# Forward substitution with a block's 32 columns spread over four groups of partitions

## The chip, the cores and the metric

The kernel runs on one core of one Trainium2 chip. The metric is device time in microseconds of one execution of the whole program. Work is done by TensorE (PE), VectorE (DVE), ScalarE (ACT), GpSimd (POOL) and SyncE (SP, which here only issues transfers); each works through its own queue in order, and they wait for one another by semaphores.

## The reference

One layer on an input of 1024 rows and 2048 columns, all in float32. A normalised input goes through one projection, whose columns feed two groups of heads; their outputs are joined, projected again, added to the input and normalised. The part that the change touches is in the gated delta rule: for every head and every chunk of 64 positions a unit lower triangular system is solved.

```python
g = -exp(a_log) * softplus(a_raw + dt_bias); beta = sigmoid(b_raw)
kb, vb = k * beta, v * beta                      # chunks of 64 positions, 8 heads of 128
gc = cumsum(g); decay = exp(gc_i - gc_j) on and below the diagonal
L = strictly_lower((kb @ k.T) * decay)           # 64 x 64 for a head and chunk
rhs = concat([vb, kb * exp(gc)])
u, w = split(triangular_solve(L + I, rhs, lower, unit_diagonal))
attn = lower((q @ k.T) * decay)
# scan over chunks, state S of 128 x 128 for a head:
v_new = u - w @ S
o = (q * exp(gc)) @ S + attn @ v_new
S = S * exp(g_last) + (k * exp(g_last - gc)).T @ v_new
```

Its result is normalised per head and gated by silu of a projected `z`. The other group of heads mixes positions in chunks of 128 by a lower triangular matrix (`sp` below).

## The kernel before

The 1024 rows are worked in two halves (`hf`) of T = 512. TensorE is the engine that everything is arranged around: each projected tile of 128 columns is an accumulator `acc` of 128x512, built from four weight chunks. A chunk of weights is loaded by SP into `wr` (`w_chunk`, three buffers, asked for three chunks ahead), ScalarE casts it to a high half `wh` (line 136), VectorE subtracts to get the low half `wl` (line 137), and TensorE multiplies high by high, high by the input's low half, and low by high (lines 238, 239 and 241): 12 matmuls of 128x512 a chunk. A finished `acc` is evicted by VectorE (line 404) into `pc` (for q, k, v), `pcz` (for z) or `pczb`.

Everything else is written as generators ("tasks"). `tick()` runs every six matmuls; a task that yields n sleeps for n ticks. Within an engine the framework then orders the instructions by its own model of when they are ready; the queues that result are fixed in the program, and some are shown below in the section on the change.

The eight heads are four pairs in each half. For a pair, `task_pair` (lines 549 to 673) does the following. The 64x64 blocks L of its heads are in DRAM (`ld`). The two 32x32 diagonal blocks of each are inverted by forward substitution: 32 blocks on 32 partitions, L in `lu`, the growing inverse in `xu` that starts as the unit matrix (lines 557 to 559, on GpSimd). Step k takes a product into `tmp` (line 566) and subtracts it (line 568), for the 31-k rows below and the k+1 columns that are not zero; each step is followed by a yield of one tick. The inverse goes to DRAM (`xd`, line 572) and back as `tn` (line 574), in pieces of one row of a block, 128 bytes. Two waits stand around the steps: W_DMA1 = 6 ticks ahead of them and W_DMA2 = 18 behind.

The full inverse follows with small matmuls (`yp`, lines 584 and 593) and transposes of `tn` (line 578) into `tt`, then `up` and `wp` (lines 606, 611), and the scan over eight chunks for both heads (matmuls `p` and `ds` at lines 621 and 632; VectorE's `vz` and `state` at 624 and 633). For each head `at` (line 649) is added to `o` by VectorE (line 650), squares and a root follow, and `swap` carries the transposed result through DRAM by GpSimd's queue (`swapo`, lines 430 and 433); VectorE's line 672 gates it. The banks of `at`, `yp`, `up`, `wp` and of the other group's `sp` (line 744, evicted by VectorE's `s`, line 746) come from one set of two (`gen_bank`), so each waits for the eviction of the last but one.

Of the kernel before, what the change touches and what calls it, by code (L numbers as in the profile page):

```python
# [8 lines left out]
F32 = mybir.dt.float32  # L9
# [3 lines left out]
ALU = mybir.AluOpType  # L13
# [4 lines left out]
P = 128  # L18
# [5 lines left out]
NT = T // P  # L24
# [7 lines left out]
def kernel(ctx, tc, x_tok, x_t, w_in, w_v0, w_vb, w_out, conv_w, norm_w, a_log, dt_bias,  # L32
                       hn_w, sgu_w, sgu_b, wsp_t, b_sp, fn_w, out):
    nc = tc.nc
# [4 lines left out]
    big = pool("big", bufs=4)  # L39
    wk = pool("wk", bufs=2)  # L40
    sm = pool("sm", bufs=2)
    dr = pool("dr", bufs=2, space=DRAM)
# [8 lines left out]
    def bc(ap, shape):  # L51
        return ap.broadcast_to(shape)
# [21 lines left out]
    for c in range(2):  # L74
        r = slice(c * 64, (c + 1) * 64)
# [374 lines left out]
    W_RSTD = 1  # L450
    RS = 4
    W_FIRST = 6
    W_DMA1 = 6
    W_DMA2 = 18
    W_GATES = 12
    W_LN = 12
    W_EM = 5
# [33 lines left out]
    def task_q(hf, h, st, pr, acc):  # L491
# [32 lines left out]
        if hh == 1:  # L524
            spawn(task_pair(hf, h // 2, st, pr))
# [23 lines left out]
    def task_pair(hf, p, st, pr):  # L549
        gt, heads = st["gt"], pr["hd"]  # L550

        ld, xd = pr["ld"], pr["xd"]
        fs = big.tile([32, 2, 32, 32], F32, tag="b8", name=f"fs{hf}_{p}")
        lu, xu = fs[:, 0], fs[:, 1]
        ldv = ld.rearrange("h t (c s j) (z i) -> s z (h t c) j i", c=2, s=2, z=2)
        for s in range(2):
            nc.gpsimd.dma_start(lu[s * 16:(s + 1) * 16], ldv[s, s])
        nc.gpsimd.memset(xu, 0.0)
        nc.gpsimd.memset(xu.rearrange("u i j -> u (i j)")[:, ::33], 1.0)
        tmp = wk.tile([32, 256], F32, tag="fst", bufs=1, name=f"fst{hf}_{p}")  # L560
        yield W_DMA1

        for k in range(31):
            n, m = 31 - k, k + 1
            tv = tmp[:, 0:n * m].rearrange("u (i j) -> u i j", j=m)
            nc.vector.tensor_tensor(tv, bc(lu[:, k, k + 1:].unsqueeze(2), [32, n, m]),  # L566
                                    bc(xu[:, k:k + 1, 0:m], [32, n, m]), op=ALU.mult)
            nc.vector.tensor_tensor(xu[:, k + 1:, 0:m], xu[:, k + 1:, 0:m], tv, op=ALU.subtract)  # L568
            yield 1
        xdv = xd.rearrange("h t (c s j) i -> s (h t c) (j i)", c=2, s=2)  # L570
        for s in range(2):
            nc.sync.dma_start(xdv[s], xu[s * 16:(s + 1) * 16].rearrange("u i j -> u (i j)"))
        tn = wk.tile([P, 2 * NT, 32], F32, tag="tn", bufs=1, name=f"tn{hf}_{p}")
        nc.sync.dma_start(tn, xd.rearrange("h t p i -> p (h t) i"))
        yield W_DMA2

        for q in range(0, P, 32):
# [3 lines left out]
        for c in range(2):  # L581
            a, b = c * 64, c * 64 + 32
# [3 lines left out]
        for c in range(2):  # L586
            b = c * 64 + 32
            nc.scalar.activation(ys[b:b + 32], yp[b:b + 32], AF.Copy, scale=-1.0)
        yield 3
        for c in range(2):  # L590
            a, b = c * 64, c * 64 + 32
# [3 lines left out]
        for c in range(2):  # L595
            a, b = c * 64, c * 64 + 32
# [78 lines left out]
    def new_pair(hf, p):  # L675
        return dict(kq=big.tile([P, 2, 2, T], F32, tag="b8", name=f"kq{hf}_{p}"),
                    ld=dr.tile([2, NT, P, 64], F32, tag="ld", name=f"ld{hf}_{p}"),
                    xd=dr.tile([2, NT, P, 32], F32, tag="xd", name=f"xd{hf}_{p}"),
                    hd=[{}, {}])

    def group_a(hf, xs, st):
        pr = [None]

        def first_done(accs):
            if hf == 0:
                late_constants()
            st["gt"] = {}
            st["rb"] = x_rows(hf)
            spawn(task_gates(hf, accs[2:6], st, st["gt"]))
            pr[0] = new_pair(hf, 0)  # L690
            spawn(task_k(hf, 0, st, pr[0], accs[0]))
            spawn(task_q(hf, 0, st, pr[0], accs[1]))
        yield from first_tiles(hf, xs, st, first_done)
        for p in range(H // 2):
            def new(p=p):
                pr[0] = new_pair(hf, p)
            jobs = [(H, task_k, 0), (0, task_q, 0), (H, task_k, 1), (0, task_q, 1), (2 * H, task_v, 0), (2 * H, task_v, 1),
                    (3 * H, task_z, 0), (3 * H, task_z, 1)]
            for ct, task, i in jobs[2 if p == 0 else 0:]:
                def done(acc, ct=ct, task=task, h=2 * p + i, first=(i == 0 and ct == H)):  # L700
                    if first:
                        new()
                    spawn(task(hf, h, st, pr[0], acc))
                yield from project(hf, ct + 2 * p + i, xs, done)
# [375 lines left out]
```

## Time and profile before

| | us |
|---|---|
| median of three runs | 1774.84 (1774.63 to 1783.69) |
| the profiled execution | 1779.21 |
| its span | 1777.5 |
| TensorE busy | 1728.8 (97%) |
| VectorE busy | 1251.7 (70%) |
| ScalarE busy | 738.5 (42%) |
| GpSimd busy | 263.6 (15%) |

The granted clock of TensorE over the whole span is 0.992 of its full speed. A 128x512 matmul lasts 0.39 us by the record, but they overlap and start every 0.227 us, so that TensorE's pace is read from starts. "Idle" is time that an engine stood, with what released it.

### The profile page before, as it was taken

To read this page: it belongs to the slowest core of one execution; us is meant where nothing else is said; L and a number is where in the kernel's file an instruction comes from. 1 tells how busy PE (TensorE), PEld (TensorE's weight loads), DVE (VectorE), ACT (ScalarE), POOL (GpSimd) and SP (SyncE) were. 2 spreads that over 40 slices of the span, in tenths; PEclk is the share of its full clock that TensorE was granted. 3 is DMA by queue.
4 is the path that set the end of the run, shared out by engine and by line. 5 is a ranking of instruction groups with operands and counts; after the bars stand their busy time and mean duration, and the time that the engine had idled before them with its cause. 6 is when DMAs were issued, how large, how long until landed. Compare 5 with 4: busy or idle time off the path is not lost.

```text
span 1777.5 us, 27441 instructions
## 1 busy us (share of the span) xinstructions
PE 1728.8 (97%) x9334; PEld 1456.6 (82%) x9334; DVE 1251.7 (70%) x2945; ACT 738.5 (42%) x1678; POOL 263.6 (15%) x314
## 2 busy tenths in 40 slices
PE   9999999999999999998999999999989999999997
PEld 8778788888997788886878878889878888888885
DVE  7798797987747633757979789793863344767765
ACT  7543544445333222646344444532422234433454
POOL 4110131211201200203012112120020000200211
PEclk9999999999999999999999999999999999999998
DMA  7455445364458734426453645444884466766455
GB/s 239 128 134 145 108 124 144 91 169 133 132 172 260 258 108 126 130 69 153 126 134 92 164 106 149 134 116 117 248 277 133 118 188 199 223 191 193 144 190 190
DMA packets 190046, 277.99 MB, mean 156 GB/s; under 512 B 38064, under 2 KB 70864, under 8 KB 189648
## 3 DMA queue, kind: packets, MB, share of 16 engines
q1 hardware_dynamic: 185216, 263.60, 50.9%
q0 software_dynamic: 4544, 12.62, 3.0%
q8 instruction: 73, 1.20, 0.3%
q14 instruction: 69, 0.57, 0.1%
q10 hardware_dynamic: 144, 0.01, 0.0%
HBM read 220.54 MB, written 55.61 MB: 155 GB/s over the span
## 4 chain that ended last, share of the span: by engine, by line
PE 54%; DVE 9%; DMA 7%; ACT 2%; issue 2%; SPq 0%; POOL 0%; DVEq 0%; ACTq 0%; POOLq 0%
PE oa L1002 12%; PE acc L238 10%; PE acc L241 10%; PE acc L239 10%; PE vb L788 7%; DMA ws<-w_out 1%; DVE wl L137 1%; DVE cv L413 1%; DMA xres<-x_tok 1%; DMA wc_d<-ws 1%; DVE c L914 1%; PE p L621 1%; PE sp L744 1%; DMA wr<-w_in 1%; PE at L649 1%
## 5 line engine op out<-in xcount | busy, mean ns | idle before, releaser
L238 PE MATMUL acc<-xh,wh 128*128 128x512 f32 x1472 | 591.8, 402 | 1.0 <-ACT wh L136 1.0
L241 PE MATMUL acc<-xh,wl 128*128 128x512 f32 x1472 | 576.9, 392 | 7.5 <-DVE wl L137 7.5
L239 PE MATMUL acc<-xl,wh 128*128 128x512 f32 x1472 | 575.8, 391 | 0.0
L136 ACT CAST wh<-wr 128x512 fp32r<-128x512 f32 x368 | 225.7, 618 | 427.7 <-PE acc L239 270.6
L137 DVE TENSOR_TENSOR wl<-wr,wh 128x512 fp32r<-128x512 f32 x368 | 258.2, 704 | 154.2 <-ACT wh L136 151.2
L241 PEld LDWEIGHTS acc<-xh,wl 128*128 128x128 f32 x1472 | 277.1, 188 | 67.0 <-DVE wl L137 9.0
L238 PEld LDWEIGHTS acc<-xh,wh 128*128 128x128 f32 x1472 | 278.0, 189 | 57.7 <-issue 3.0
L239 PEld LDWEIGHTS acc<-xl,wh 128*128 128x128 f32 x1472 | 278.0, 189 | 51.5 <-issue 0.2
L1002 PE MATMUL oa<-who,a 128*128 128x512 f32 x864 | 267.9, 390 | 0.2 <-ACT who L136 0.2
L1002 PEld LDWEIGHTS oa<-who,a 128*128 128x128 f32 x864 | 162.6, 188 | 34.7 <-ACT who L136 0.6
L1002 PE MATMUL oa<-wlo,a 128*128 128x512 f32 x432 | 168.7, 390 | 0.6 <-DVE wlo L137 0.5
L137 DVE TENSOR_TENSOR wlo<-wro,who 128x512 fp32r<-128x512 f32 x108 | 79.4, 738 | 52.7 <-ACT who L136 52.2
L413 DVE SCALAR_TENSOR_TENSOR cv<-pc,cw,cv 128x511 f32<-128x511 f32 (+1 forms) x144 | 109.1, 758 | 9.6 <-ACT cv L410 8.2
L788 PE MATMUL vb<-whvb,xh 128*128 128x256 f32 x384 | 110.5, 288 | 0.0
L788 PE MATMUL vb<-wlvb,xh 128*128 128x256 f32 x384 | 108.6, 283 | 0.0
L788 PE MATMUL vb<-whvb,xl 128*128 128x256 f32 x384 | 108.6, 283 | 0.0
L136 ACT CAST who<-wro 128x512 fp32r<-128x512 f32 x108 | 66.6, 618 | 96.6 <-PE oa L1002 63.7
L1002 PEld LDWEIGHTS oa<-wlo,a 128*128 128x128 f32 x432 | 81.3, 188 | 18.5 <-DVE wlo L137 1.7
L566 DVE TENSOR_TENSOR fst<-fs 32x31 f32<-32x31 f32 (+15 forms) x248 | 89.3, 360 | 4.3
L568 DVE TENSOR_TENSOR fs<-fs,fst 32x31 f32<-32x31 f32 (+15 forms) x248 | 89.0, 359 | 4.1
L625 ACT ACTIVATE o<-p,g_egs 64x128 f32<-64x128 f32 x128 | 46.5, 363 | 84.3 <-DVE vz L624 81.6
L952 POOL TENSOR_TENSOR c<-c,fw 128x512 f32<-128x512 f32 x24 | 37.6, 1596 | 254.6 <-ACT sqh L950 254.6
(245 smaller groups left out, 2379.2 us busy)
## 6 DMA issues: line engine op xcount, KB each, us to landing
wr<-w_in SPq DMA_DIRECT2D x368, 256.0 KB, 3.3
ws<-w_out SPq DMA_DIRECT2D x64, 256.0 KB, 4.0
wc_d<-ws SPq DMA_DIRECT2D x64, 256.0 KB, 3.6
wro<-wc_d SPq DMA_DIRECT2D x64, 256.0 KB, 2.8
ar<-mix_d SPq DMA_DIRECT2D x56, 256.0 KB, 3.5
wrvb<-w_vb SPq DMA_DIRECT2D x48, 256.0 KB, 2.7
wro<-w_out SPq DMA_DIRECT2D x48, 256.0 KB, 2.8
xr<-x_t SPq DMA_DIRECT2D x32, 256.0 KB, 4.2
```

The lines of the kernel that those rows point to most:

```text
L136: nc.scalar.copy(hi, src)
L137: nc.vector.tensor_tensor(lo, src, hi.bitcast(F32), op=ALU.subtract)
L238: nc.tensor.matmul(acc, hi[:, kk, :], xh, start=(k == 0), stop=False)
L239: nc.tensor.matmul(acc, hi[:, kk, :], xl, start=False, stop=(last and lo is None))
L241: nc.tensor.matmul(acc, lo[:, kk, :], xh, start=False, stop=last)
L413: nc.vector.scalar_tensor_tensor(cv[:, s:], acc[:, :T - s], w, cv[:, s:], op0=ALU.mult, op1=ALU.add)
L566: nc.vector.tensor_tensor(tv, bc(lu[:, k, k + 1:].unsqueeze(2), [32, n, m]), bc(xu[:, k:k + 1, 0:m], [32, n, m]), op=ALU.mult)
L568: nc.vector.tensor_tensor(xu[:, k + 1:, 0:m], xu[:, k + 1:, 0:m], tv, op=ALU.subtract)
L625: nc.scalar.activation(hd["o"][ra, t, :], pp[rq, :], AF.Copy, scale=gt["egs"][rq, h, t:t + 1])
L788: nc.tensor.matmul(a, l[:, tsl], r[:, k % 2, :], start=fl, stop=sp_, skip_group_check=True)
L952: nc.gpsimd.tensor_tensor(c, c, env["fw"][q], op=ALU.mult)
L1002: nc.tensor.matmul(acc[t], l[:, tsl], r[:, 0, :], start=fl, stop=sp_, skip_group_check=True)
```

## The change

A block's 32 columns are spread over four groups of 32 partitions: column j = 4m+g lies on group g at place m, so that all four groups do one instruction together, and step k treats k//4+1 places instead of k+1 columns. For that the blocks L are loaded four times, once a group, half of the loads by GpSimd's queue and half by SP's; the unit matrix is set by a memset of 128 partitions and four for the diagonals. Steps go two to a tick. The inverse is written by one transfer of 128x256 and read back in pieces of eight elements, 32 bytes; it lies in `tn` by groups, and its readers take it through a view with a stride. W_DMA1 is 9 and W_DMA2 is 24.

```diff
--- before.py
+++ after.py
@@ -450,8 +450,8 @@
     W_RSTD = 1
     RS = 4
     W_FIRST = 6
-    W_DMA1 = 6
-    W_DMA2 = 18
+    W_DMA1 = 9
+    W_DMA2 = 24
     W_GATES = 12
     W_LN = 12
     W_EM = 5
@@ -549,29 +549,32 @@
     def task_pair(hf, p, st, pr):
         gt, heads = st["gt"], pr["hd"]
 
+
         ld, xd = pr["ld"], pr["xd"]
-        fs = big.tile([32, 2, 32, 32], F32, tag="b8", name=f"fs{hf}_{p}")
-        lu, xu = fs[:, 0], fs[:, 1]
+        fs = big.tile([P, 2, 32, 32], F32, tag="b8", name=f"fs{hf}_{p}")
+        lu, xu = fs[:, 0], fs[:, 1, 0:8].rearrange("u a (b m) -> u (a b) m", m=8)
         ldv = ld.rearrange("h t (c s j) (z i) -> s z (h t c) j i", c=2, s=2, z=2)
-        for s in range(2):
-            nc.gpsimd.dma_start(lu[s * 16:(s + 1) * 16], ldv[s, s])
-        nc.gpsimd.memset(xu, 0.0)
-        nc.gpsimd.memset(xu.rearrange("u i j -> u (i j)")[:, ::33], 1.0)
-        tmp = wk.tile([32, 256], F32, tag="fst", bufs=1, name=f"fst{hf}_{p}")
+        xf = xu.rearrange("u i m -> u (i m)")
+        nc.gpsimd.memset(xf, 0.0)
+        for g in range(4):
+            for s in range(2):
+                (nc.gpsimd, nc.sync)[g % 2].dma_start(lu[g * 32 + s:(g + 1) * 32:2], ldv[s, s])
+            nc.gpsimd.memset(xf[g * 32:(g + 1) * 32, 8 * g:8 * g + 33 * 7 + 1:33], 1.0)
+        tmp = wk.tile([P, 80], F32, tag="fst", bufs=1, name=f"fst{hf}_{p}")
         yield W_DMA1
 
         for k in range(31):
-            n, m = 31 - k, k + 1
+            n, m = 31 - k, k // 4 + 1
             tv = tmp[:, 0:n * m].rearrange("u (i j) -> u i j", j=m)
-            nc.vector.tensor_tensor(tv, bc(lu[:, k, k + 1:].unsqueeze(2), [32, n, m]),
-                                    bc(xu[:, k:k + 1, 0:m], [32, n, m]), op=ALU.mult)
+            nc.vector.tensor_tensor(tv, bc(lu[:, k, k + 1:].unsqueeze(2), [P, n, m]),
+                                    bc(xu[:, k:k + 1, 0:m], [P, n, m]), op=ALU.mult)
             nc.vector.tensor_tensor(xu[:, k + 1:, 0:m], xu[:, k + 1:, 0:m], tv, op=ALU.subtract)
-            yield 1
-        xdv = xd.rearrange("h t (c s j) i -> s (h t c) (j i)", c=2, s=2)
-        for s in range(2):
-            nc.sync.dma_start(xdv[s], xu[s * 16:(s + 1) * 16].rearrange("u i j -> u (i j)"))
-        tn = wk.tile([P, 2 * NT, 32], F32, tag="tn", bufs=1, name=f"tn{hf}_{p}")
-        nc.sync.dma_start(tn, xd.rearrange("h t p i -> p (h t) i"))
+            if k % 2 == 0:
+                yield 1
+        nc.sync.dma_start(xd, xf)
+        tn = wk.tile([P, 4, 2 * NT, 8], F32, tag="tn", bufs=1, name=f"tn{hf}_{p}")
+        nc.sync.dma_start(tn, xd.rearrange("(g u c s) (r m) -> (c s r) (g u) m", g=4, s=2, c=2, m=8))
+        tn = tn.rearrange("p g u m -> p u m g")
         yield W_DMA2
 
         for q in range(0, P, 32):
@@ -675,7 +678,7 @@
     def new_pair(hf, p):
         return dict(kq=big.tile([P, 2, 2, T], F32, tag="b8", name=f"kq{hf}_{p}"),
                     ld=dr.tile([2, NT, P, 64], F32, tag="ld", name=f"ld{hf}_{p}"),
-                    xd=dr.tile([2, NT, P, 32], F32, tag="xd", name=f"xd{hf}_{p}"),
+                    xd=dr.tile([P, 256], F32, tag="xd", name=f"xd{hf}_{p}"),
                     hd=[{}, {}])
 
     def group_a(hf, xs, st):
```

(Three lines more stand in the file ahead of the steps, so that line 566 becomes 569, 568 becomes 571, 649 becomes 652, 672 becomes 675 and 746 becomes 749.)

The change moves instructions on the queues. First VectorE, at the first pair's first step in the first half, before; `acc_24` and `acc_25` are two tiles of z, `wl_25_0` is the low half of the first chunk for `acc_25`, `fs` and `fst` are the substitution's.

```order
L568 TENSOR_TENSOR fs_0_1229<-fs_0_1229,fst_0_1234 32x28x4
L566 TENSOR_TENSOR fst_0_1234<-fs_0_1229 32x135
L137 TENSOR_TENSOR wl_25_2_1375<-wr_25_2_1372,wh_25_2_1374 128x512
L568 TENSOR_TENSOR fs_0_1229<-fs_0_1229,fst_0_1234 32x27x5
L566 TENSOR_TENSOR fst_0_1234<-fs_0_1229 32x156
L568 TENSOR_TENSOR fs_0_1229<-fs_0_1229,fst_0_1234 32x26x6
L566 TENSOR_TENSOR fst_0_1234<-fs_0_1229 32x175
L568 TENSOR_TENSOR fs_0_1229<-fs_0_1229,fst_0_1234 32x25x7
L566 TENSOR_TENSOR fst_0_1234<-fs_0_1229 32x192
L404 TENSOR_TENSOR pcz_0_1392<-acc_24_1299,rb_715 128x512
L568 TENSOR_TENSOR fs_0_1229<-fs_0_1229,fst_0_1234 32x24x8
L137 TENSOR_TENSOR wl_25_3_1401<-wr_25_3_1398,wh_25_3_1400 128x512
```

The same place after the change:

```order
L425 STREAM_TRANSPOSE pc_17_1293<-cv_17_1295 128x4x4x32
L404 TENSOR_TENSOR pcz_0_1401<-acc_24_1308,rb_715 128x512
L569 TENSOR_TENSOR fst_0_1243<-fs_0_1229 128x31
L571 TENSOR_TENSOR fs_0_1229<-fs_0_1229,fst_0_1243 128x31
...
L569 TENSOR_TENSOR fst_0_1243<-fs_0_1229 128x52
L571 TENSOR_TENSOR fs_0_1229<-fs_0_1229,fst_0_1243 128x26x2
L569 TENSOR_TENSOR fst_0_1243<-fs_0_1229 128x50
L571 TENSOR_TENSOR fs_0_1229<-fs_0_1229,fst_0_1243 128x25x2
L569 TENSOR_TENSOR fst_0_1243<-fs_0_1229 128x48
L137 TENSOR_TENSOR wl_25_0_1326<-wr_25_0_1323,wh_25_0_1325 128x512
```

The eviction of `acc_24` stood among the later steps, behind `wl_25_2`; it now stands ahead of the first step, and 15 of the steps' instructions stand between it and `wl_25_0`.

Between `wl_25_0` and `wl_25_1` there are 19 of them; the end of that stretch, after the change:

```order
L569 TENSOR_TENSOR fst_0_1243<-fs_0_1229 128x75
L571 TENSOR_TENSOR fs_0_1229<-fs_0_1229,fst_0_1243 128x15x5
L137 TENSOR_TENSOR wl_25_1_1356<-wr_25_1_1353,wh_25_1_1355 128x512
L569 TENSOR_TENSOR fst_0_1243<-fs_0_1229 128x70
L137 TENSOR_TENSOR wl_25_2_1382<-wr_25_2_1379,wh_25_2_1381 128x512
L571 TENSOR_TENSOR fs_0_1229<-fs_0_1229,fst_0_1243 128x14x5
L137 TENSOR_TENSOR wl_25_3_1412<-wr_25_3_1409,wh_25_3_1411 128x512
```

The two chunks' low halves were next to each other but for one transpose; the rest of the four now follows within two small instructions.

On ScalarE the silu `z_0` of `pcz_0` stood behind the four casts for `acc_25` and now stands ahead of them.

Second SP's queue, before, around the chunk `wr_25_0` (`swapv` carries v through DRAM, `ld` the blocks L):

```order
L187 DMA wr_24_3_1293<-w_in 128x512
L515 DMA ld_0_759<-gl_1_1215 128x4x64
L432 DMA swapv_0_1236<-pc_16_1163 32x4x128 x4
L187 DMA wr_25_0_1318<-w_in 128x512
L187 DMA wr_25_1_1350<-w_in 128x512
L187 DMA wr_25_2_1372<-w_in 128x512
L433 DMA pc_16_1163<-swapv_0_1236 128x512
L187 DMA wr_25_3_1398<-w_in 128x512
```

There `ld` was followed by the four transfers of `pc_16` and by three chunks. And after:

```order
L187 DMA wr_24_3_1302<-w_in 128x512
L515 DMA ld_0_759<-gl_1_1215 128x4x64
L432 DMA swapv_0_1245<-pc_16_1163 32x4x128 x2
L561 DMA fs_0_1229<-ld_0_759 16x32x32 x4
L432 DMA swapv_0_1245<-pc_16_1163 32x4x128 x2
L187 DMA wr_25_0_1323<-w_in 128x512
L432 DMA swapv_1_1336<-pc_17_1293 32x4x128 x2
L433 DMA pc_16_1163<-swapv_0_1245 128x512
L432 DMA swapv_1_1336<-pc_17_1293 32x4x128 x2
L187 DMA wr_25_1_1353<-w_in 128x512
L187 DMA wr_25_2_1379<-w_in 128x512
L187 DMA wr_25_3_1409<-w_in 128x512
```

The four loads of L stand behind `ld`, whose data they read, and the transfers of `pc_17` now stand ahead of `wr_25_1`.

## Rows read from the trace of the kernel before

**Rows 1.** The head of the page: span, then busy time of each engine

```profile
span 1777.5 us, 27441 instructions
...
PE 1728.8 (97%) x9334; PEld 1456.6 (82%) x9334; DVE 1251.7 (70%) x2945; ACT 738.5 (42%) x1678; POOL 263.6 (15%) x314
```

**Rows 2.** TensorE's waits: line waited for, us in total, times, longest us

```profile
PE at L649 <- DVE s L746: 10.7, 2, 5.6
PE acc L241 <- DVE wl L137: 7.5, 3, 5.6
PE ds L632 <- DVE vz L624: 4.0, 10, 0.9
```

**Rows 3.** Windows: length, busy us of PE, PEld, DVE, ACT, POOL; PEclk, DMA share, GB/s

```profile
114.00:150.00 36.00, 36.00 (x161) 29.80 (x160) 34.29 (x85) 9.95 (x17) 2.08 (x2) 1.00 0.41 110
308.00:334.00 26.00, 24.90 (x133) 20.27 (x131) 22.34 (x60) 13.33 (x34) 5.53 (x6) 1.00 0.40 104
574.00:580.00 6.00, 0.44 (x2) 0.01 (x1) 4.08 (x7) 1.14 (x2) 0.00 (x0) 0.74 0.90 306
580.00:584.00 4.00, 3.93 (x14) 3.52 (x15) 2.81 (x5) 0.91 (x5) 1.66 (x1) 0.53 0.77 232
```

**Rows 4.** The substitution's second line, all of it, then by form (busy us, mean ns)

```profile
L568 DVE TENSOR_TENSOR fs<-fs,fst 32x31 f32<-32x31 f32 (+15 forms) x248 | 89.0, 359 | 4.1
...
L568 DVE TENSOR_TENSOR fs<-fs,fst 32x87 f32<-32x87 f32 x16 | 3.6, 225 | 0.2
...
L568 DVE TENSOR_TENSOR fs<-fs,fst 32x31 f32<-32x31 f32 x16 | 3.0, 188 | 0.3
```

**Rows 5.** Time line of TensorE around 116 us: start us, duration us, instruction

```profile
115.99 0.39 PE L238 MATMUL acc<-xh,wh 128*128 128x512 f32 x1
...
116.44 0.39 PE L241 MATMUL acc<-xh,wl 128*128 128x512 f32 x1
```

**Rows 6.** Time line of VectorE, 113 to 121 us

```profile
113.81 0.69 DVE L137 TENSOR_TENSOR wl<-wr,wh 128x512 fp32r<-128x512 f32 x1 [0.40 <-ACT wh L136]
114.42 0.17 DVE L566 TENSOR_TENSOR fst<-fs 32x31 f32<-32x31 f32 x1
114.62 0.20 DVE L568 TENSOR_TENSOR fs<-fs,fst 32x31 f32<-32x31 f32 x1
114.86 1.08 DVE L566 TENSOR_TENSOR fst<-fs 32x60 f32<-32x60 f32 x1
...
120.19 0.67 DVE L404 TENSOR_TENSOR pcz<-acc,rb 128x512 f32<-128x512 f32 x1
```

**Rows 7.** Time line of TensorE at 580 us; the idle time before is in brackets

```profile
580.07 2.05 PE L649 MATMUL at<-ut,gae 128*128 128x128 f32 x8 [5.63 <-DVE s L746]
```

**Rows 8.** Time line of VectorE, 554 to 580 us

```profile
554.35 0.68 DVE L650 TENSOR_TENSOR o<-o,at 128x512 f32<-128x512 f32 x1
...
577.91 0.75 DVE L672 SCALAR_TENSOR_TENSOR o<-ut,hnw,z 128x512 f32<-128x512 f32 x1 [1.59 <-DMA ut<-swapo]
...
579.18 0.74 DVE L746 SCALAR_TENSOR_TENSOR s<-sp,lnw,brow 128x512 f32<-128x512 f32 x1
```

**Rows 9.** DMA issues: count, KB each, median us from issue to landing

```profile
wr<-w_in SPq DMA_DIRECT2D x368, 256.0 KB, 3.3
...
swapo<-ut POOLq DMA_DIRECT2D x64, 64.0 KB, 3.5
ut<-swapo POOLq DMA_DIRECT2D x16, 256.0 KB, 3.9
...
xd<-fs SPq DMA_DIRECT2D x16, 64.0 KB, 2.1
tn<-xd SPq DMA_DIRECT2D x8, 128.0 KB, 4.7
```

**Rows 10.** Time line of SP's queue near 107 us

```profile
106.64 1.87 SPq L187 DMA_DIRECT2D wr<-w_in  x3
```

**Rows 11.** The tile tn: duration ns min/median/max, first and last start us

```profile
L578 DVE STREAM_TRANSPOSE tt<-tn x32: 415/435/442, 157.3 to 1209.4; 32x256 f32<-32x256 f32 x32
```

## What the change does to the time: the prediction

> **What bounds the kernel now.** I read the profile's head first, then the waits of TensorE, then windows, then single stretches of the time lines. The head says that TensorE is busy for 1728.8 us of a span of 1777.5 and VectorE for 1251.7 [rows 1]. So whatever the change saves on VectorE counts only where TensorE waits for VectorE. The waits show three such causes of any size: the product `at` behind the eviction `s` (10.7 us in two waits), the third matmul of a weight chunk behind its low half `wl` (7.5 us in three), and the scan's `ds` behind `vz` (4.0 us in ten) [rows 2]. The windows tell where there is nothing to win: during the substitution of the first pair (114 to 150 us) TensorE is busy for 36.00 of 36 us although VectorE has 34.29 us of work. In a stretch with a scan, 308 to 334, TensorE lacks 1.1 us of 26 [rows 3]. [...]
>
> **What the substitution costs and will cost.** Its second line, L568, has 248 instructions of 89.0 us, and the first, with as many of the same sizes, I take alike: 178 us. An instruction of 31 elements takes 188 ns and one of 87 elements 225, while the mean is 359 [rows 4]: nearly all of the small one is a price per instruction. After the change a step has k//4+1 columns, so 8 to 76 elements instead of 31 to 256. With 0.20 to 0.23 us for each, 496 instructions are 99 to 114 us against 178: 64 to 79 us less on VectorE. By the 36.00 of 36 [rows 3] TensorE gets none of that directly. It could get some where steps lie beside a scan: at most the 1.1 us of each of the six scans that have a following pair's steps (pairs 0 to 2 in two halves), 6.6 us in all. After the change the next pair's first step stands behind the scan, but an earlier start of the scan brings one more conv of VectorE beside it, so I take half: -3 us (0 to -7).
>
> **What the shorter substitution moves.** Two steps in a tick and other waits make a pair 9+16+24 = 49 ticks instead of 6+31+18 = 55. A tick is six matmuls at a pitch of 0.227 us, 115.99 to 116.44 being two pitches [rows 5], so 1.36 us: everything behind the substitution comes about 8 us earlier. The order of VectorE's work then changes, and here I see the main cost. In the first pair, the substitution begins now at 114.42 us, before the eviction `pcz_0` at 120.19 [rows 6]; `wl_25_0` and `wl_25_1` are done by then. After the change the longer first wait puts the first step behind `pcz_0`, and then 15 steps' instructions stand on VectorE ahead of `wl_25_0`. `pcz_0` reads `acc_24`, whose last matmul is the one before 115.99 [rows 5]; VectorE thus can't begin the 15 before that, though TensorE wants `wl_25_0` for its third matmul at 116.44 [rows 5].
>
> Worked out: the last matmul of `acc_24` ends near 116.2. An instruction of 512 elements holds the next one up by 0.61 us (113.81 to 114.42) [rows 6], so `pcz_0` has passed at 116.8. The pitch of a small step's instruction is 0.20 to 0.24 us (114.42, 114.62, 114.86) [rows 6]; the 1.08 us of the next row is a single delay, not a step's price; I take 0.24 since most of the 15 have about 50 elements: 3.6 us, to 120.4. `wl_25_0` takes 0.69 [rows 6], so 121.1: TensorE waits 4.65 us (4.0 with 0.20 us per step). Behind it 19 more instructions of up to 76 elements stand ahead of `wl_25_1`. With 0.26 us each (225 ns at 87 elements [rows 4], and a gap of 0.04 as above) it ends at 120.4+0.6+4.9+0.7 = 126.6. TensorE wanted it at 116.44+12x0.227 = 119.2. The first half therefore loses 7.4 us by there. The second half has the same order with 12 instructions before `wl_25_0` and 18 between it and `wl_25_1`: by the same prices 6.5 us. Together +14 us (10 with 0.20 us throughout, 18 if the clock drops for longer than the second wait lasts).
>
> The wait is long enough to touch the clock. Behind the wait of 5.63 us before 580.07 [rows 7] the granted clock was 0.53 for 4 us [rows 3], a loss of 1.9 us. In the new place that loss lies inside the second wait (126.6 minus 121.1 minus 2.7 us of matmuls leaves 2.8), so I add nothing. ScalarE's `z_0` also comes ahead of the cast `wh_25_0` now, but its path from `pcz_0` is shorter than the 15 steps, so it doesn't decide.
>
> In pairs 1 to 3 `pcz` and some ten small instructions stand ahead of `wl` of the second next chunk, where a chunk's 2.7 us lie between: 0.6+10x0.22+0.7 = 3.5 us after VectorE reaches `pcz`, and VectorE reaches it up to 0.9 us late, against a need 3.6 us after the last matmul. 0 to 1.5 us at each of six places; I take 0.5, +3 us (0 to +9).
>
> **The two long waits at the halves' ends.** TensorE stands for 5.63 us before 580.07 [rows 7]. The transfers of `swapo` and its return hold VectorE's in-order queue at L672 until 577.91, and `s` stands two places behind it [rows 8]. After the change the fourth pair is earlier and `at` of both heads comes before `sp`; the next product that needs a bank freed behind the return is the third `sp`, 95 large and 16 small matmuls after the first `at`, about 23.4 us. The chain from `at` to that `s` took some 26.7 us (eviction of `at` at 554.35 [rows 8], `s` done at 579.9). So a wait of 3 to 6 us stays: I take 0.75 us off at each half's end, -1.5 us (bounds: both waits and the clock behind them gone, 2x7.5 = -15; each 2.5 us longer, +5).
>
> **The transfers.** Eight reads of 1024 pieces of 128 B each (`tn`) take 4.7 us to land [rows 9] and become 4096 pieces of 32 B. The writes of half as many bytes in long rows land in 2.1 [rows 9], so at most 2.6 us of the 4.7 are due to the pieces; four times the pieces add 0 to 7.8 us. The wait of 24 ticks, 33 us, covers the reader. What could suffer are weights issued behind: `wr_25_0` was issued at 106.64 [rows 10] and first used at 115.99 [rows 5], 9.3 us, of which landing (3.3 [rows 9]), cast and subtraction need 4.7. Spare 4.7; I take 0 (0 to +25, that is eight times 3.1). [...]
>
> The four copies of the blocks are eight issues instead of two, four of them on SP behind `ld`, which pushes `wr_25_0` back by some 2.5 us (three issues there take 1.87 us [rows 10]); that is less than the spare and, in the first pair, far less than the wait through VectorE. On GpSimd, which is busy 263.6 us of the span [rows 1], two more issues and a larger memset per pair have idle time around them. The transposes now read `tn` with a stride; they are 32 instructions of 0.435 us [rows 11], and double would be 14 us of VectorE outside any wait listed [rows 2].
>
> **The sum.** +14 (first pairs) +3 (others) -3 (scans) -1.5 (ends of halves) +0 = +12.5 us. The profiled execution took 1779.21 us, its span 1777.5; that is 4.4 above the median of 1774.84 shown. Against its own time it would be 1791.7, and against the median 1787, which I predict.
>
> **The rivals.** *The gains offset the waits*: the new order costs its lower 10, other pairs nothing, and a good part of the ends' waits goes. For it: the wait at L649 has 10.7 us to give [rows 2], and the chain behind it is mostly two transfers, which vary. Against: TensorE's position there moves with the chain. 10-7-3 = 0, so 1775, from 1768 to 1783. *Faster*, one mechanism: at both ends of the halves the bank is free when the third `sp` comes, since the transfers of `swapo` take their median of 3.5 and 3.9 us [rows 9] rather than what they took there; both waits and the clock behind them go, -15. It decides from about 4 us less of that chain at each end. With the scans' -6.6 and the first pairs' +10 that is -12, so 1763. Against: DMA's share is 0.90 in that window [rows 3]. *The 32-byte pieces* hold the queues and every readback delays a chunk: +25 on top of +12.5, 1812; against: the spare above. *The change doesn't give VectorE its time back*, because a step's price is per instruction: then the pitch stays near 0.36 us, the first pairs' waits become 20 us, 1797; against: the 188 and 225 ns [rows 4].
>
> **How the numbers follow.** Forecast 0.55 (its own range 1780 to 1796), offset 0.27, faster 0.08, pieces 0.06, no saving 0.04. The range 1766 to 1800 leaves out the faster case, the pieces and the forecast's tail, under 2 in 10. A change of 0.5% is 8.9 us, about what a measurement of this kernel tells from none: faster is below 1766, slower above 1783.7. Faster 0.09; same 0.33 (all of the offset, a tenth of the forecast); slower 0.58.
>
> **What would show it.** In the changed profile: a wait of TensorE of 4 to 5 us near 116 to 121 us for `wl`, its like in the second half, and a lower clock behind them; VectorE's busy time 64 to 79 us less with TensorE's idle time larger; waits at `sp` in place of those at L649; small waits for `wl` near the end of each pair's `acc_26`, `acc_28` and `acc_30`. If no such wait at 116 us is there, the main step is wrong; if the time is below 1775 it was outweighed by the ends of the halves; if the chunks behind `tn` land late, the pieces decide.

## The result, and the profile after

The changed kernel takes 1824.09 us (median; 1821.1 to 1827.3), the kernel before 1776.31 in the same runs: ratio 1.0261, 95% interval 1.0226 to 1.0296. That is 48 us slower, where +12.5 us and a range up to 1800 us were forecast. The direction was right, the size was a quarter of what came.

The head of the page after, which answers to [rows 1]:

```profile
span 1825.6 us, 27577 instructions
...
PE 1745.8 (96%) x9334; PEld 1470.3 (81%) x9334; DVE 1205.8 (66%) x2945; ACT 738.6 (40%) x1678; POOL 269.2 (15%) x354
```

The span grew by 48.1 us: TensorE is 17.0 us longer busy and 31.1 us longer idle. VectorE's busy time fell by 46 us, and none of it reached TensorE. The waits of TensorE after, which answer to [rows 2] (line waited for, us in total, times, longest):

```profile
PE acc L241 <- DVE wl L137: 14.9, 9, 3.3
PE sp L747 <- DVE s L749: 12.8, 2, 6.6
PE ds L635 <- DVE vz L627: 9.8, 13, 2.2
PE up L609 <- ACT ut L611: 9.2, 4, 3.5
PE acc L238 <- ACT wh L136: 4.9, 3, 2.0
PE yp L596 <- ACT ys L591: 4.8, 4, 2.1
```

`wl` went from 7.5 to 14.9 us, `ds` from 4.0 to 9.8, the wait at the halves' ends moved from `at` to `sp` (10.7 to 12.8), and three waits are new in this size: `up` for `ut`, `yp` for `ys`, and the first matmul of a chunk for its cast `wh`. The waits for `wl` and `wh` lie in good part at the first pair of each half; those at `ds`, `up` and `yp` lie in what follows a pair's steps, called its tail below. The windows after (columns as in [rows 3]):

```profile
114.00:130.00 16.00, 10.31 (x35) 7.25 (x34) 12.54 (x43) 2.99 (x5) 2.63 (x4) 0.79 0.40 113
596.00:612.00 16.00, 9.39 (x33) 7.58 (x32) 7.64 (x13) 1.86 (x3) 3.87 (x4) 0.68 0.88 286
868.00:882.00 14.00, 8.55 (x28) 5.96 (x27) 10.78 (x36) 3.31 (x6) 2.33 (x4) 0.88 0.41 112
```

The stretches around 116 and 870 us are the first pairs of the two halves; from 596 to 612 is the end of the first half. In each TensorE stands and the granted clock is lowered for a while: its mean is 0.79, 0.68 and 0.88 in the three windows. Over the whole span the granted clock is 0.985 against 0.992.

The two lines of the substitution, which answer to [rows 4] (busy us, mean ns):

```profile
L571 DVE TENSOR_TENSOR fs<-fs,fst 128x60 f32<-128x60 f32 (+24 forms) x248 | 60.4, 243 | 5.4
L569 DVE TENSOR_TENSOR fst<-fs 128x60 f32<-128x60 f32 (+24 forms) x248 | 56.0, 226 | 4.5
```

116.4 us instead of 178: 62 us less, where 64 to 79 were forecast. The strided transposes took 6.5 us of that back (below); the other 10 us that VectorE's busy time didn't fall by weren't taken apart.

### The profile page after: what moved, and what is told of

Read it like the earlier page. It is cut to its first block, busy times and chain, and to the rows that moved or that the text cites. A ratio compares the mean times of both kernels' runs of the same rounds, so it can differ in the third digit from the quotient of the medians.

```text
span 1825.6 us, 27577 instructions
## 1 busy us (share of the span) xinstructions
PE 1745.8 (96%) x9334; PEld 1470.3 (81%) x9334; DVE 1205.8 (66%) x2945; ACT 738.6 (40%) x1678; POOL 269.2 (15%) x354
## 4 chain that ended last, share of the span: by engine, by line
PE 63%; DVE 14%; DMA 13%; issue 4%; ACT 4%; SPq 1%; POOL 0%; DVEq 0%; ACTq 0%; POOLq 0%
PE oa L1005 12%; PE acc L238 12%; PE acc L241 12%; PE acc L239 11%; PE vb L791 6%; DVE wl L137 2%; DMA ws<-w_out 2%; DMA pc<-swapk 2%; DMA pc<-swapq 2%; DMA wc_d<-ws 2%; DVE cv L413 1%; PE ds L635 1%; DMA swapk<-pc 1%; PE p L624 1%; DVE fst L569 1%
## 5 line engine op out<-in xcount | busy, mean ns | idle before, releaser
L241 PE MATMUL acc<-xh,wl 128*128 128x512 f32 x1472 | 581.7, 395 | 15.1 <-DVE wl L137 14.9
L791 PEld LDWEIGHTS vb<-whvb,xh 128*128 128x128 f32 x384 | 73.6, 192 | 0.3
L791 PEld LDWEIGHTS vb<-wlvb,xh 128*128 128x128 f32 x384 | 73.6, 192 | 0.1
```

The costliest lines, as they stand in the source:

```text
L241: nc.tensor.matmul(acc, lo[:, kk, :], xh, start=False, stop=last)
L791: nc.tensor.matmul(a, l[:, tsl], r[:, k % 2, :], start=fl, stop=sp_, skip_group_check=True)
```

## The experiments

Where it was lost over time can be read by lining up the starts of the same weight chunk's first matmul in both time lines. The table gives the lag behind the kernel before, in us, worked out from those starts, for the change and for six of the runs below. Each column is a single execution; the one of the kernel before took 1779.21 us, 3 us above its median.

```
first matmul of               before at   change  ticks  layout  no SP   +blocks  composite  ys on
                              us                   alone  alone   loads             VectorE
wr_24_0 (half 1, pair 1)      105.11       0.1     0.0   -0.2    -1.1     0.3      -0.1       0.8
wr_10_0 (after pair 1's z)    126.87       8.4     0.0    8.6    -1.1     0.3      -0.1       0.8
wr_13_0 (pair 2's k behind)   258.32       5.6    -2.0    9.6    -4.0    -0.4      -3.6      -2.7
wr_43_0 (half 1, tails past)  628.36      29.0     0.9   16.3     8.7     6.7       0.6      -0.2
wr_24_0 (half 2, pair 1)      833.36      26.4    -2.8   16.0     5.9     6.7      -0.9      -2.0
wr_10_0 (after pair 1's z)    855.15      34.4    -2.8   24.4     5.9     6.7       0.0      -2.0
wr_42_0 (half 2, tails past) 1332.63      50.4     4.1   36.9    19.6    14.6      11.4       4.7
```

The change loses 8.4 and 8.0 us in the two first pairs, and 20.6 and 16.0 us from there past the tails of each half (less 2.6 where a wait near 823 us became shorter).

**Where the loads of L are issued.** Theory A: the four loads on SP wait there for `ld`, and what stands behind them, weights and v's transfers, comes later. Theory B: the tail's earlier place, which the ticks bring. Theory C: the stride of the readers of `tn`. The first run takes the loads off SP:

```diff
-                (nc.gpsimd, nc.sync)[g % 2].dma_start(lu[g * 32 + s:(g + 1) * 32:2], ldv[s, s])
+                nc.gpsimd.dma_start(lu[g * 32 + s:(g + 1) * 32:2], ldv[s, s])
```

> The changed kernel (1824 us) with all eight loads of the blocks L on GpSimd's queue, none on SP's. Theory A (the loads on SP's queue, which wait there for ld, push the weights and the transfers of v back, and VectorE's order follows): the 8 us that each half loses at its first pair and the 0.5 to 1 us at each later pair's wl come back, about 22 us, so 1802 us; no wait of TensorE at 116 to 127 us. Theory B (the tail of each pair comes 8 us earlier and runs into waits of the next pair): nothing changes, 1820 to 1826.

Measured: 1795.96 us, ratio 1.0114 (1.0093 to 1.0135). 28 us are back. The windows of that run at the first pairs (in its second half 22 us earlier) and its largest waits:

```profile
114.00:130.00 16.00, 16.00 (x72) 13.28 (x71) 6.24 (x10) 5.19 (x9) 4.98 (x9) 1.00 0.65 174
846.00:860.00 14.00, 14.00 (x64) 11.59 (x63) 5.76 (x9) 5.95 (x9) 5.53 (x11) 1.00 0.74 196
```

```profile
PE sp L747 <- DVE s L749: 13.5, 2, 6.9
PE ds L635 <- DVE vz L627: 9.9, 11, 2.3
PE up L609 <- ACT ut L611: 7.9, 4, 2.7
PE acc L241 <- DVE wl L137: 5.2, 3, 4.1
```

TensorE is busy for 16.00 of 16 us and for 14.00 of 14 with the same two steps a tick and the same wait of 9 ticks. So the first pairs' waits don't come from the ticks. VectorE's queue stands there again as in the kernel before: `wl_25_0` and the two chunks behind it ahead of the eviction `pcz_0`. The last of the three and the eviction:

```profile
114.31 0.69 DVE L137 TENSOR_TENSOR wl<-wr,wh 128x512 fp32r<-128x512 f32 x1 [0.87 <-ACT wh L136]
115.05 0.69 DVE L404 TENSOR_TENSOR pcz<-acc,rb 128x512 f32<-128x512 f32 x1
```

In both halves, all twelve kernels without a load on SP (the one before and eleven runs) have three low halves ahead of that eviction, the two with two loads have one, and the four with four loads have none.

A run with two of the eight loads on SP:

```diff
+                (nc.sync if g == 1 else nc.gpsimd).dma_start(lu[g * 32 + s:(g + 1) * 32:2], ldv[s, s])
```

> The changed kernel with two of the eight loads of L on SP and six on GpSimd; with none on SP it took 1796 us, with four 1824. Theory A (a dose: each load on SP pushes what is behind it): between them, 1805 to 1815, the wait near 118 us shorter than 3 us. Rival (a step: the waits for weights appear only when VectorE's queue has all low halves behind the eviction, which four loads bring and two do not): 1796 to 1802.

Measured: 1804.4 us, ratio 1.0159 (1.0139 to 1.0178): 8 us for two loads, 28 for four. That lies just below the dose's range and above the rival's, so theory A holds as a dose, but it isn't even: the second two cost more than the first. At the first pair TensorE stands once, 1.84 us, and there the reason is a chunk of weights that comes late. SP issues `wr_25_1` behind the transfers of v at 115.11 (in the run without loads on SP at 106.26), it lands at 120.17, and its cast and first matmul follow:

```profile
115.11 2.27 SPq L187 DMA_DIRECT2D wr<-w_in  x3
...
120.25 1.90 ACT L136 CAST wh<-wr 128x512 fp32r<-128x512 f32 x3 [2.49 <-DMA wr<-w_in]
...
120.92 0.50 PE L238 MATMUL acc<-xh,wh 128*128 128x512 f32 x1 [1.84 <-ACT wh L136]
```

And the loads alone, in the kernel before:

```diff
-            nc.gpsimd.dma_start(lu[s * 16:(s + 1) * 16], ldv[s, s])
+            nc.sync.dma_start(lu[s * 16:(s + 1) * 16], ldv[s, s])
```

> The kernel before with its two loads of the blocks L on SP's queue instead of GpSimd's, nothing else. Theory A (a load on SP waits there for ld, and what is queued behind it, the weights and the transfers of v, comes later): TensorE waits for weights near 116 to 125 us and at the like place of the second half, 3 to 8 us each, 1783 to 1793 us. Rival (the loads on SP cost only together with the new layout or ticks): 1774 to 1779.

Measured: 1778.52 us, ratio 1.0019 (1.0008 to 1.003): 3 us, so the rival held in size. Its first pair loses 4.5 us near 118 to 126 us, and by 628 us that is given back. Two loads on SP are cheap with the old steps, dearer with the new layout, and four are dear.

**The ticks, and the layout alone.** The ticks of the change in the kernel before (waits 9 and 24, two steps a tick):

```diff
-    W_DMA1 = 6
-    W_DMA2 = 18
+    W_DMA1 = 9
+    W_DMA2 = 24
...
-            yield 1
+            if k % 2 == 0:
+                yield 1
```

> The kernel before with the ticks of the changed one alone (two steps a tick, waits of 9 and 24), blocks on 32 partitions, two loads on GpSimd as before. Theory A: no loss at the first pairs, 1770 to 1780. Theory B: the tail is 8 us early, about 25 us lost in pairs 1 to 3: 1800.

Measured: 1780.91 us, ratio 1.0024 (1.0009 to 1.0039). In the old layout the earlier tail costs 4 us, not 25. The reverse, the new layout with the old ticks, is that diff turned around on the changed kernel:

> The changed kernel's layout with the ticks of before (one step a tick, waits of 6 and 18 ticks). Theory A: the loads stay on SP, so the first pairs still lose 8 us a half: 1815 to 1824. Theory B: the tail is back at its place, the 25 us lost in pairs 1 to 3 come back: about 1798, and the waits of up for ut (9.2 us) go to about 1 us. Theory C (the price of reading the inverse with a stride): yp's pitch stays 57 ns instead of 32, some 6 us that neither recovers.

Measured: 1815.39 us, ratio 1.0218 (1.0195 to 1.0241). The first pair loses its 8.6 us with the old ticks too. But 9 us of the change are back: with four loads on SP the old ticks lose 7.7 instead of 20.6 us in the first half's tails and 12.5 instead of 16.0 in the second's. And the tail put back by a longer second wait, with two steps a tick kept:

```diff
-    W_DMA2 = 24
+    W_DMA2 = 30
```

> The changed kernel with the second wait at 30 ticks instead of 24, so that a pair has 55 ticks as before and its tail comes where it came. Theory B: some 25 us come back, 1799. Theory A: 1820 to 1826, the first pairs' waits as they are.

Measured: 1830.59 us, ratio 1.0307 (1.0274 to 1.034). Nothing came back, so it isn't the tail's place: theory B falls. What of the old ticks gives the 9 us, the shorter first wait or one step a tick, wasn't taken apart. The old ticks without loads on SP (theory D: there the earlier tail costs, since the inverse is late):

> The changed kernel with all loads of L on GpSimd and the ticks of before (one step a tick, waits 6 and 18). Theory D (the earlier tail costs where the inverse is late: up's waits for ut, 7.9 us, and the longer waits at sp): those go, 1780 to 1786. Rival (the earlier tail costs nothing, as the kernel before with these ticks, 1781 against 1777, has it nearly): 1793 to 1799.

Measured: 1800.55 us, ratio 1.0143 (1.0122 to 1.0164), against 1.0114 with the new ticks, so without those loads the old ticks cost 5 us instead of giving 9. Theory D falls: `up`'s waits for `ut` shrink from 7.9 to 1.1 us there, but `yp` then waits 14.6 us for `ys`.

**The stride.** Columns dealt in blocks leave the inverse in rows (all loads on GpSimd). The run has two more differences: steps of up to 192 elements, and a readback in four transfers.

```diff
-            nc.gpsimd.memset(xf[g * 32:(g + 1) * 32, 8 * g:8 * g + 33 * 7 + 1:33], 1.0)
+            nc.gpsimd.memset(xf[g * 32:(g + 1) * 32, 64 * g:64 * g + 9 * 7 + 1:9], 1.0)
...
-            n, m = 31 - k, k // 4 + 1
+            n, m = 31 - k, min(k + 1, 8)
...
-        tn = wk.tile([P, 4, 2 * NT, 8], F32, tag="tn", bufs=1, name=f"tn{hf}_{p}")
+        tn = wk.tile([P, 2 * NT, 32], F32, tag="tn", bufs=1, name=f"tn{hf}_{p}")
+        for g in range(4):
+            nc.sync.dma_start(tn[:, :, 8 * g:8 * g + 8],
+                              xd[g * 32:(g + 1) * 32].rearrange("(u c s) (r m) -> (c s r) u m", s=2, c=2, m=8))
```

> The changed kernel with all loads of L on GpSimd (1796 us in an earlier run), and the columns dealt in blocks, column 8g+m on group g, so that the inverse is read back (in four transfers, still pieces of 32 bytes) into rows without a stride; steps have up to 192 elements instead of 76. Theory C (the stride is what is left to pay): yp's pitch falls from 57 to 32 ns, 6 us, and the transposes from 638 to 435 ns; 1784 to 1790. Rival (what is left is the 32-byte pieces or the tail's earlier place): 1793 to 1799.

Measured: 1787.85 us, ratio 1.0069 (1.0049 to 1.0089), 8 us less than with the stride. The readers of `tn` in the change, then in this run (duration ns min/median/max; the transposes answer to [rows 11]):

```profile
L587 PE MATMUL yp<-tn,gl x256: 218/229/231, 174.7 to 1266.5; 32*32 32x32 f32 x128
L581 DVE STREAM_TRANSPOSE tt<-tn x32: 620/638/652, 145.5 to 1246.0; 32x256 f32<-32x256 f32 x32
```

```profile
L588 PE MATMUL yp<-tn,gl x256: 184/191/257, 168.3 to 1232.9; 32*32 32x32 f32 x128
...
L582 DVE STREAM_TRANSPOSE tt<-tn x32: 424/435/445, 168.2 to 1223.3; 32x256 f32<-32x256 f32 x32
```

A group of 32 of the matmuls in TensorE's time line, in the kernel before and in the change:

```profile
284.13 1.09 PE L584 MATMUL yp<-tn,gl 32*32 32x32 f32 x32
```

```profile
282.91 1.76 PE L587 MATMUL yp<-tn,gl 32*32 32x32 f32 x32
```

A matmul of 32 columns on a moving operand (the matmul's second input, here `tn`) with a stride takes 229 ns, instead of 191 in the kernel before and in this run, and the group of 32 takes 1.76 us instead of 1.09: 8 x 0.67 = 5.3 us on TensorE. The rest of the 8 us wasn't taken apart. A transpose takes 638 ns instead of 435, 6.5 us on VectorE. Neighbours in `tn` lie 64 elements apart in the change and next to each other in this run.

**The 32-byte pieces**, alone, in the kernel before:

```diff
-        nc.sync.dma_start(tn, xd.rearrange("h t p i -> p (h t) i"))
+        for g in range(4):
+            nc.sync.dma_start(tn[:, :, 8 * g:8 * g + 8], xd.rearrange("h t p i -> p (h t) i")[:, :, 8 * g:8 * g + 8])
```

> The kernel before, with the inverse read back in pieces of 32 bytes (four transfers of 1024 pieces each instead of one of 1024 pieces of 128 bytes), nothing else. If the pieces cost by themselves: 1783 us or more, chunks of weights behind them landing over 2 us later. Rival (covered): 1773 to 1779.

Measured: 1775.91 us, ratio 1.0001 (0.9991 to 1.0011). They cost nothing here: the four transfers land in 4.3 us each (median of 32), the one with pieces of 128 bytes in 4.7. The readback of the change lands as fast as before [rows 9] (median us to landing):

```profile
tn<-xd SPq DMA_DIRECT2D x8, 128.0 KB, 4.2
```

**Eight loads on GpSimd**, alone, in the kernel before; the three more copies fill partitions that no one reads:

```diff
+        for g in range(1, 4):
+            for s in range(2):
+                nc.gpsimd.dma_start(fs[g * 32 + s * 16:g * 32 + (s + 1) * 16, 0], ldv[s, s])
```

> The kernel before with each block of L loaded four times on GpSimd's queue (eight loads of 64 KB a pair instead of two; the three more copies are not used), the used ones last. If the later start of the steps and GpSimd's held queue are what is left of the loss (12 us in the version with loads on GpSimd, columns in blocks and old ticks): 1783 to 1790. Rival (GpSimd has time for it): 1773 to 1779.

Measured: 1776.8 us, ratio 1.0021 (1.0005 to 1.0036). That is 1 to 6 us by the interval, little but not nothing.

**What is left.** Loads on GpSimd, blocks, and the ticks of before:

> All three undone: loads on GpSimd, columns in blocks without a stride, ticks of before; what stays is 128 partitions with smaller steps and pieces of 32 bytes. If A, C and D are the whole of the loss: 1770 to 1777, not slower than before, with VectorE's busy time 30 to 60 us less. If the pieces of 32 bytes or the eight loads cost by themselves: 1782 or more.

Measured: 1787.0 us, ratio 1.0073 (1.0054 to 1.0092). By its trace it was ahead of the kernel before by 5.6 us late in the second half, and lost 14 us behind that, 12 of them in the tails of the second and third pair. The composite with early steps (first wait 9, two steps a tick) and the tail at its old place (second wait 30):

> The composite that the runs point to: loads of L on GpSimd, columns in blocks without a stride, two steps a tick, and a second wait of 30 ticks, so that the steps are over early and the tail stands where it stood before. If the waits of yp for ys (9.9 us in the version with old ticks) came from the inverse being late: 1768 to 1778, the best of the versions on 128 partitions. Rival (the remaining loss is not in the ticks): 1784 to 1790.

Measured: 1789.52 us, ratio 1.0084 (1.0066 to 1.0102). So some 12 to 14 us are left without SP's loads and the stride, with the ticks of before or with the tail at its old place. The composite's time lines at one tail of the second half, ScalarE and then TensorE (the idle time before and its releaser are in brackets):

```profile
1009.64 0.72 ACT L410 ACTIVATE cv<-pc,cw 128x512 f32<-128x512 f32 x1
1015.56 0.31 ACT L441 ACTIVATE sqk<-pc 128x128 f32<-128x128 f32 x1 [5.20 <-DMA pc<-swapk]
...
1017.36 0.76 ACT L592 ACTIVATE ys<-yp 32x256 f32<-32x256 f32 x2
```

```profile
1009.42 1.09 PE L588 MATMUL yp<-tn,gl 32*32 32x32 f32 x32
...
1018.18 1.51 PE L597 MATMUL yp<-tt,ys 32*32 32x32 f32 x32 [3.36 <-ACT ys L592]
```

ScalarE stands for 5.20 us at `sqk`, the squares of the next pair's k, which wait for its transfer; `ys`, for which TensorE waits, is queued behind them. In the kernel before, ScalarE's queue has `ys` behind one of the four squares at the like place of the second pair, here behind three:

```profile
1011.27 1.09 PE L584 MATMUL yp<-tn,gl 32*32 32x32 f32 x32
...
1015.82 0.31 ACT L441 ACTIVATE sqk<-pc 128x128 f32<-128x128 f32 x1 [0.65 <-DMA pc<-swapk]
...
1016.25 0.76 ACT L588 ACTIVATE ys<-yp 32x256 f32<-32x256 f32 x2
...
1017.06 1.09 PE L593 MATMUL yp<-tt,ys 32*32 32x32 f32 x32 [0.40 <-ACT ys L588]
```

Counted from the start of the first product, `ys` came after 4.98 us there and after 7.94 here. 1.6 of these 3.0 us are the transfer of k, behind which the squares began after 4.55 and 6.14 us; the rest is what stands between, two more squares and a cast. Theory E: `ys` off that queue brings the time back.

```diff
-            nc.scalar.activation(ys[b:b + 32], yp[b:b + 32], AF.Copy, scale=-1.0)
+            nc.vector.tensor_scalar(ys[b:b + 32], yp[b:b + 32], -1.0, None, op0=ALU.mult)
```

> The composite (1789.5 us: loads on GpSimd, blocks, two steps a tick, second wait 30) with the negated copy ys taken by VectorE instead of ScalarE. Theory E (ScalarE's queue holds ys behind the squares sqk of the next pair, which wait there for the k transfer): the waits of yp for ys, 11.3 us in four, go, and with them part of the lower clock: 1773 to 1779. Rival (ys is late for another reason, its inputs or the banks): 1787 to 1792.

Measured: 1781.25 us, ratio 1.0029 (1.0012 to 1.0045). 8 of the 14 us are back. That is short of the 1773 to 1779 forecast, so theory E holds for a good half; the wait for `ys` is gone and one for `tt` is in its place:

```profile
PE at L653 <- DVE s L750: 10.8, 2, 6.0
PE up L610 <- DVE tt L601: 6.5, 4, 2.6
PE acc L241 <- DVE wl L137: 5.3, 2, 4.2
```

The same edit with the ticks of before:

> The version with loads on GpSimd, blocks and the ticks of before (1787 us), with ys on VectorE. Theory E: the waits of yp for ys, 9.9 us, go: 1772 to 1778. Rival: 1785 to 1789.

Measured: 1781.76 us, ratio 1.004 (1.0023 to 1.0057): 5 of 12 us back, again less than forecast. In the change itself it was `ut` that stood behind the squares:

```profile
299.24 0.31 ACT L441 ACTIVATE sqk<-pc 128x128 f32<-128x128 f32 x1 [5.07 <-DMA pc<-swapk]
...
301.34 0.59 ACT L611 COPY ut<-up 128x512 f32<-128x512 f32 x1
```

```diff
-            nc.scalar.copy(ut, upp)
+            nc.vector.tensor_copy(ut, upp)
```

> The changed kernel (1824 us) with the copy ut taken by VectorE instead of ScalarE, nothing else. Theory E: the waits of up for ut, 9.2 us in four, go, 1810 to 1817. Rival: 1820 to 1828.

Measured: 1827.22 us, ratio 1.0299 (1.0264 to 1.0333). The waits for `ut` are gone, but `wp` for `wq` grew from 0.4 to 5.8 us and `ds` from 9.8 to 11.2: a miss. With `ys` and `ut` both on VectorE, blocks, loads on GpSimd and the ticks of the change:

> The version with loads on GpSimd, blocks and the ticks of the change (1788 us), with ys and ut on VectorE. Theory E: the waits for ut (3.5 us) go, those at sp (12.5 us) stay: 1780 to 1785. Rival: 1786 to 1791.

Measured: 1796.37 us, ratio 1.0123 (1.0089 to 1.0157), 8 us slower than without the two edits. A miss too: `ds` waits 11.2 us for VectorE there. No version of this layout beat the kernel before.

## Why the prediction was wrong

**The step that failed** is the part of the sum for all that lies behind the first pairs: +3 (others), -3 (scans) and -1.5 (ends of halves), together -1.5 us, where about +34 came. Three things were left out of it: 13 us go with the new loads on SP, which a pair of sentences costed at nothing ("which pushes `wr_25_0` back by some 2.5 us", "that is less than the spare"); 5.3 us are TensorE's own reading with a stride, which had no term; and the other 16 or so lie in the order of the tails, which the runs explain in part. The pair of sentences on the loads failed at the first pairs too. The push of that one chunk was 3.8 us and did stay within the spare of 4.7:

```profile
103.33 0.43 SPq L515 DMA_DIRECT2D ld<-gl  x1
...
106.52 2.68 SPq L561 DMA_DIRECT2D fs<-ld  x4
...
110.43 0.39 SPq L187 DMA_DIRECT2D wr<-w_in  x1
```

`wr_25_0` was issued at 110.43 instead of 106.64, and landed at 113.96 by the trace, 2 us before TensorE was done with the chunk ahead. But the next chunk, `wr_25_1`, behind the transfers of v, was issued at 114.81 instead of 107.12, 7.7 us later, and I had priced the first alone; in the run with two loads on SP that is the whole wait of the first pair. And the four loads came with another order on ScalarE and VectorE, and that order made the waits of the change:

```profile
116.99 0.63 ACT L544 ACTIVATE z<-pcz 128x512 f32<-128x512 f32 x1 [5.24 <-DVE pcz L404]
117.52 0.60 ACT L136 CAST wh<-wr 128x512 fp32r<-128x512 f32 x1
```

```profile
116.26 0.69 DVE L404 TENSOR_TENSOR pcz<-acc,rb 128x512 f32<-128x512 f32 x1 [3.77 <-PE acc L241]
116.87 1.02 DVE L569 TENSOR_TENSOR fst<-fs 128x31 f32<-128x31 f32 x1
...
121.14 0.21 DVE L569 TENSOR_TENSOR fst<-fs 128x48 f32<-128x48 f32 x1
121.26 0.69 DVE L137 TENSOR_TENSOR wl<-wr,wh 128x512 fp32r<-128x512 f32 x1
...
126.58 0.24 DVE L571 TENSOR_TENSOR fs<-fs,fst 128x75 f32<-128x75 f32 x1
126.74 0.68 DVE L137 TENSOR_TENSOR wl<-wr,wh 128x512 fp32r<-128x512 f32 x1
```

```profile
118.17 0.64 PE L238 MATMUL acc<-xh,wh 128*128 128x512 f32 x1 [1.95 <-ACT wh L136]
...
122.00 0.80 PE L241 MATMUL acc<-xh,wl 128*128 128x512 f32 x1 [2.76 <-DVE wl L137]
...
127.48 0.50 PE L241 MATMUL acc<-xh,wl 128*128 128x512 f32 x1 [0.98 <-DVE wl L137]
```

I had read that order and the wait that it forces, and put it down to the longer first wait of 9 ticks. The runs say otherwise: the ticks alone don't bring it, the layout with the old ticks does, and the loads on GpSimd take it away with ticks unchanged. That the scheduler chooses this order because its model has the chunks late behind a load that waits is an inference; what is shown is that the loads' queue decides.

**Point by point.**
- First pairs: +14 forecast, 8.4 + 8.0 = 16.4 measured. First half 7.4 against 8.4. The steps' pitch was 0.24 us, the 15 instructions took from 116.87 to 121.26 (the first of them 1.02 us), and the second low half was ready at 127.4, not 126.6. The loss by the lower clock lay inside the second wait, as said: the granted clock was 0.50 from 118.5 to 125.0 us, and 0.98 us of that wait was left. `z_0` did decide the first matmul (1.95 us, for the cast behind it), though not the sum. Right in size, wrong in its cause.
- Pairs 1 to 3 and the tails: +3 - 3 - 1.5 forecast, about +34 measured (20.6 + 16.0 - 2.6). This term was mis-sized most. Of it 13 us go with SP's loads (the same two stretches lose 23.5 us without them: 9.8 and 13.7). The stride has 5.3 us of TensorE in it, which I gave no term at all: I priced its transposes and overlooked that `yp` reads `tn` as its moving operand. For the rest the runs show a part: 5 to 8 us go with `ys` behind the next pair's squares, measured in versions without SP's loads and stride, and the old ticks give 9 us back while the loads are on SP. That other links of the tail in in-order queues hold what remains is not shown; in the change itself, `ut` off the squares' queue gave nothing back.
- Scans: a gain of 3 was forecast; `ds` waits for `vz` 9.8 us instead of 4.0. In the run of the ticks alone it waits 8.1 us; in the layout with the old ticks it waits 2.0, but there `p` waits 11.0 us for `state` instead of 0.9. So the longer wait at `ds` comes with the ticks; that it is other work of VectorE beside the scan is not shown. The bound (0 to -7) excluded a loss, and had no reason to.
- Halves' ends: -1.5 forecast. TensorE waits 12.8 us instead of 10.7, at `sp` as said.
- Transfers: 0 for the pieces was right (1.0001): in the run of the pieces alone the readback lands no later (4.3 us against 4.7). The choice of the queue for the loads was worth 28 us (1824.09 against 1795.96), through what waits behind the load.
- VectorE's saving: 62 us on the two lines, just below the 64 to 79, and 46 on VectorE as a whole, where the prediction named 64 to 79 as the sign. Nearly right, and worth nothing to TensorE directly, as said.
- A slip in the rivals: the 1797 of the last one is counted from the profiled execution (1779.21 and 18.5); from the median, as the others are, it is 1793.

**What stays open.** 28 us go with the loads on SP, 8 with the stride, 8 with `ys` behind the squares. These differences come from runs taken one on top of the other, and they needn't add up in another sequence. The 9 us that the old ticks give back belong to the layout with loads on SP alone. The last 5 us (1.0029) weren't taken apart; the eight loads on GpSimd can be some of them. Why four loads cost more than twice what two do isn't settled beyond the orders given above.

## What to carry to other kernels

Where engines work in order, as here, a cheap instruction is priced by what stands behind it: four loads put on the queue that feeds the weights, which stood there 0.6 us for their own input at the first pair and took 2.68 us to issue, came with the weights behind them 3.8 and 7.7 us later and with another order of two other engines. So after a change read each queue around the places where it waits, and test the suspicious queue by moving the load alone. Work saved on an engine that isn't the bound bought nothing by itself here: VectorE was busy for 46 us less, and TensorE stood 31.1 us longer. And look at what stands in front of the links that the bound waits for: in the composite it was three squares instead of one, and `ys` came after 7.94 us instead of 4.98.

## What the runs showed of the hardware

A matmul on a moving operand of 32 float32 columns whose neighbours lie 64 elements apart takes TensorE 229 ns in the change, instead of 191 in the kernel before (a group of 32 takes 1.76 us instead of 1.09), and VectorE's 32x256 transpose of the same tile 638 ns instead of 435. A readback in 4096 pieces of 32 bytes lands in 4.2 us in the change (median of eight), no later than one in 1024 pieces of 128 bytes in the kernel before, 4.7 us [rows 9].
